# Layer 1's expert blocks staggered on TensorE, and the expert features regrouped so that gate and up rows load in runs of eight

## The chip, the cores and the metric

One core of a Trainium2 chip runs the whole program in one launch. The metric is device time in microseconds (us), the median of three runs. The engines are TensorE (PE; its weight loads are listed apart as PEld), VectorE (DVE), ScalarE (ACT), GpSimd (POOL) and SyncE (SP), whose queue issues nearly all loads. Sixteen DMA engines move the data.

## The reference, cut to what matters

Two transformer layers run on 256 image tokens and, in layer 0, on 256 context tokens as well (D = 1024, everything in float32). Each layer is: modulation, attention, residual and layer norm, then a mixture of 16 experts of which each token uses two. Only the mixture concerns this change:

```
h2    = x * (1 + sc2) + sh2                      # tokens x 1024
gates = top-2 of the best group of 4 experts, normalised   # tokens x 16
g     = h2 @ w_gate[e]                           # 1024 -> 512, per expert
u     = h2 @ w_up[e]                             # 1024 -> 512
a     = silu(g) * u * gate[token, e]
out  += a @ w_down[e]                            # 512 -> 1024
x     = layer_norm(ALPHA * x + g2 * out)
```

The sums over the 1024 features of `g` and `u` may be taken in any order, as long as h2 and the rows of `w_gate` and `w_up` are ordered alike.

## The kernel before, in words

**Slots and blocks.** Experts have fixed capacities. Three experts of each layer are static, the others are sorted by their count of tokens into dynamic slots whose expert number is read from a register when its weights are loaded. A slot is cut into blocks of R = 128, 64 or 32 rows. Layer 1 has fifteen blocks, in this order: e0, e1, e2 (32 rows each, static), d0 (a block of 128 and one of 64), d7 and d9 (32 each), d4 and d3 (64 each), d2 (64 and 32), d1 (128), d5 (64), d8 and d6 (32 each). The number after the d is the slot's index.

**One block in layer 1.** `pick` (L1285) gathers a group's rows, up to 128, out of h2 by a one-hot product into `xt`, features on the partitions. `hidden` then does three things: the products with gate and up, 8 feature chunks (L1235, or L1216 and L1218 where R is 128); a copy of the result out of PSUM to `gu` (L1238) and its transposes (L234); and silu times up on ACT and DVE (L1244 to L1246), which gives `aT`. `down` (L1264, or L1258) multiplies `aT` by `w_down`. `put_out` (L1300 to L1302) scales the rows and splits them into `yh` and `yl`, and `put` (L1320, L1323) adds them to the tokens' residual `xs` by a one-hot product and DVE additions, two token tiles of two halves each, over two PSUM buffers. Below, P stands for the products of a block, T for its transposes, D for its down product.

**Their order.** `step` runs P and T of a block, then `flush`, which does the whole put of the block before, then D, and keeps its own put for the next step. In the code that is: P(i), T(i), put(i-1), D(i), P(i+1), and so on. Tile, the layer that turns this program into engine streams, decides the order on each engine from the order of the code and from an estimate of when each instruction can run, so that an instruction may move ahead of an earlier one that is not ready by that estimate.

**Weights.** An expert's weights are six tiles of 1 MB (gate 2, up 2, down 2), loaded by SP (`expert_load`, L155) into a ring, twelve tiles in layer 1. A load waits until the tile that was loaded twelve before it has been read for the last time, and loads are issued strictly in order. With rows `(k p)`, a partition takes from DRAM one row of 2 KB per feature chunk of gate and up, and one row of 4 KB per chunk of down. The first three experts of layer 1 are loaded early, during its attention.

**h2.** `out_proj` makes h2 by two DVE operations on 128x1024 (L873: subtract the mean, times a row; L879: times the deviation, plus a row). Layer 0 writes h2 to DRAM for gathers, layer 1 splits it into two parts in SBUF. The routing's own operations stand on DVE behind and between them (L875, L876, L885).

Of the kernel before, what the change touches and what calls it, by code (L numbers as in the profile page):

```python
# [142 lines left out]
class K:  # L143
# [686 lines left out]
    def out_proj(self, l, ts, w, oT, rows, h2d, score):  # L830
        nc, wk = self.nc, self.wkb
        for n, t in [(n, t) for n in range(2) for t in ts]:
            c = t // 2
            g1, G2, B2 = [rows[:, 3 * c + i] for i in range(3)]
            cs = slice(512 * n, 512 * n + 512)
            zs = []
            if n:
                zs.append(self.half_T(self.xs[:, t, 0:512], 0))
                bs = self.sm.tile([P, 2, 6], F32, name="bs", tag="bs")
                nc.vector.bn_stats(bs[:, 0], self.xs[:, t, 0:512])  # L840
            ps = self.psum([P, 512], "acc")
# [24 lines left out]
            mv = self.sm.tile([P, 6], F32, name="mv5", tag="mv5")  # L866
            nc.vector.bn_aggr(mv[:, 0:2], bs)
            self.rstd(mv[:, 2:3], mv[:, 1:2], 1, 1e-5)
            nc.vector.tensor_scalar(mv[:, 3:4], mv[:, 0:1], -1.0, None, op0=ALU.mult)

            z = self.xs[:, t, :]
            h2 = wk.tile([P, D], F32, name="h2", tag="h2")
            nc.vector.scalar_tensor_tensor(h2, z, mv[:, 0:1], G2, op0=ALU.subtract, op1=ALU.mult)  # L873
            sc = score[:, t, :]
            nc.vector.scalar_tensor_tensor(sc, bl[:, c, 1], mv[:, 3:4], ps, op0=ALU.mult, op1=ALU.add)  # L875
            nc.vector.scalar_tensor_tensor(sc, sc, mv[:, 2:3], bl[:, c, 0], op0=ALU.mult, op1=ALU.add)  # L876

            e = nc.scalar.activation(sc, sc, AF.Exp, scale=-1.0)
            nc.vector.scalar_tensor_tensor(h2, h2, mv[:, 2:3], B2, op0=ALU.mult, op1=ALU.add)  # L879
            if l == 0:  # L880
                nc.scalar.dma_start(h2d[P * t:P * t + P, :], h2)
            else:
                nc.scalar.copy(self.h2s[0][:, t], h2)
                nc.vector.tensor_sub(self.h2s[1][:, t], h2, self.h2s[0][:, t])
            nc.vector.tensor_scalar(sc, sc, 1.0, None, op0=ALU.add)  # L885
            nc.vector.reciprocal(sc, sc)
            nc.vector.tensor_mul(mv[:, 4:5], mv[:, 3:4], mv[:, 2:3])
            nc.scalar.activation(z, z, AF.Identity, scale=mv[:, 2:3], bias=mv[:, 4:5])
            if last:
                i = nc.scalar.activation(self.junk, self.nhalf[:, 0:1], AF.Sigmoid)  # L890
                self.tc.add_manual_dep(i.ins, e.ins.name, NOSYNC, reason="behind the exponentials")
# [283 lines left out]
    def expert_load(self, l, kind, i):  # L1175
        nc, a = self.nc, self.a
        out = []
        if kind == "d":
            v = nc.sync.value_load(self.ids[0:1, i:i + 1], min_val=0, max_val=NE - 1)
        for nm in ("w_gate", "w_up", "w_down"):  # L1180
            K = 4 if nm == "w_down" else 8
            if kind == "s":
                src = a[nm][l][CAPS[l]["first"] + i].rearrange("(k p) f -> p k f", p=P)
            else:
                src = a[nm][l][bass.ds(v, 1)].rearrange("o (k p) f -> p (o k) f", p=P)
            out.append(self.wload(src, K, 4096 // K))
        return out

# [17 lines left out]
            nc.any.tensor_copy(xt[:, k0:k0 + kb, :], pt)  # L1206
        return xt

    def hidden(self, xt, R, gate, up):

        nc, ep = self.nc, self.ep
        aT = ep.tile([P, 4, R], F32, name="aT", tag="aT")
        if R == 128:
            pg, pu = self.psum([P, 512]), self.psum([P, 512])
            for k in range(8):
                nc.tensor.matmul(pg, xt[:, k, :], gate(k), start=k == 0, stop=k == 7)  # L1216
            for k in range(8):
                nc.tensor.matmul(pu, xt[:, k, :], up(k), start=k == 0, stop=k == 7)  # L1218
            sg = ep.tile([P, 512], F32, name="sg", tag="sg")
            nc.scalar.activation(sg, pg, AF.Sigmoid)  # L1220
            nc.vector.tensor_mul(sg, sg, pg)
            nc.vector.tensor_mul(sg, sg, pu)
            pt = self.psum([P, 4, P], "tr")
            for k in range(4):
                self.tr(pt[:, k, :], sg[:, P * k:P * k + P])
            nc.any.tensor_copy(aT, pt)
            return aT
        W = 8 * R
        q = 512 // W
        ps = self.psum([P, W])  # L1230
# [5 lines left out]
                                 start=k == 0, stop=k == 7, tile_position=(0, R * j), skip_group_check=True)  # L1236
        gu = ep.tile([P, W], F32, name="gu", tag="gu")
        nc.any.tensor_copy(gu, ps)  # L1238
        n = W // P
        pt = self.psum([P, n, 2, q, R], "tr")  # L1240
        for i in range(n):
# [63 lines left out]
    def put(self, ys, R, tok, T):  # L1305
# [5 lines left out]
        dt = self.sp.tile([P, nj, P * T], F32R, name="dt", tag="dt", bufs=1)  # L1311
        for j in range(nj):
            nc.vector.tensor_scalar(dt[:, j], self.const("iota")[:, 0:P * T], tok, m[:, j:j + 1], op0=ALU.is_equal, op1=ALU.mult)
        for t in range(T):
            for n in range(2):
                ps = self.psum([P, 512], "c")
                w = min(W, 512)
                for c in range(512 * n, 512 * n + 512, w):
                    for i in range(2):
                        nc.tensor.matmul(ps[:, c % 512:c % 512 + w], dt[:, c // W, P * t:P * t + P], ys[i][:, c % W:c % W + w],  # L1320
                                         start=i == 0, stop=i == 1, skip_group_check=True)
                x = self.xs[:, t, 512 * n:512 * n + 512]
                nc.vector.tensor_add(x, x, ps)  # L1323

    def moe(self, l, T, h2d, yd, rp, prep):

# [18 lines left out]
        def run(part):  # L1345
            for kind, i, cap in part:
                wg, wu, wd = self.expert_load(l, kind, i)
                for r0, R in cut(cap):
# [4 lines left out]
                        self.hold = g.ins.name  # L1353
                    xt = self.xgT(xg, R)
                    y, out = self.rows_out(R)
                    aT = self.hidden(xt, R, wg, wu)
                    self.down(aT, R, wd, out)
                    self.scatter(y, z, R, yd, NT)
                    b[0] += 1
# [1 line left out]
        def groups(part):  # L1361
# [9 lines left out]
                    n += R  # L1371
            return out

        todo, held = [], []

        def run1(grs, xt0=None, last=False):

            for g in grs:
# [4 lines left out]
                for sc, r0, R, load in g:  # L1383
                    todo.append((xt[:, :, o:o + R], R, load))
                    o += R
            while last and todo:
                step()
            if last:
                flush()

        def step():
            xt, R, load = todo.pop(0)
            if load:
                self.w1 = early.pop(0) if early else self.expert_load(l, *load)
            wg, wu, wd = self.w1
            aT = self.hidden(xt, R, wg, wu)
            flush()
            x, z = [v[:, b[0]:b[0] + 1] for v in ixs]
            b[0] += 1
            y, out = self.put_out(R, z)  # L1400
            self.down(aT, R, wd, out)
            held.append((y, R, x))

        def flush():
            while held:
                self.put(*held.pop(0), T)

        NS = NE - ndyn(l)
        early = [self.expert_load(l, *s[:2]) for s in slots[:NS]] if l else []
# [48 lines left out]
    def overflow(self, l, T, h2d, yd, prep):  # L1458
# [8 lines left out]
        with tc.If(v > 0):  # L1467
# [3 lines left out]
            with tc.For_i(0, NE, 1) as e, tc.tile_pool(name=f"ov{l}", bufs=2) as vp:  # L1471
                fl = vp.tile([1, T], I32, name="fl")
                nc.sync.dma_start(fl, fid[bass.ds(e, 1)])
                for b in range(T):
                    fv = nc.values_load(fl[0:1, b:b + 1], min_val=0, max_val=512)
                    with tc.If(fv > 0):
# [29 lines left out]
                        def part(nm):  # L1506
                            kp = 4 if nm == "w_down" else 8
                            n = 4096 // kp
                            s = a[nm][l][bass.ds(e, 1)].rearrange("o (k p) f -> p (o k) f", p=P)

                            def get(k):
                                w = self.ep.tile([P, n], F32, name="wv" + nm, tag="xt" if kp == 4 else "gu")
                                nc.sync.dma_start(w, s[:, k, :])
                                return w
                            return get
                        aT = self.hidden(xt, P, part("w_gate"), part("w_up"))
                        wd = part("w_down")
                        y, out = self.rows_out(P) if l == 0 else self.put_out(P, ix[1])
                        pss = [self.psum([P, 512]) for _ in range(2)]
# [6 lines left out]
                        if l == 0:  # L1526
                            self.scatter(y, ix[1], P, yd, NT)
                        else:
                            self.put(y, P, ix[0], T)

    def combine_load(self, t, T, yd):
        NT = P * T
# [267 lines left out]
```

## Time and profile before

| | |
|---|---|
| time, median of 3 runs (lowest to highest) | 1067.28 us (1066.06 to 1070.09) |
| the profiled execution: its own time, its span | 1065.16 us, 1063.4 us |
| PE busy | 972.4 us, 91% of the span |
| DVE, ACT busy | 498.5 us (47%), 260.6 us (25%) |
| loads by SP's queue | 267.08 MB, 68.0% of the 16 DMA engines' span |
| mean granted TensorE clock | 0.975 of full speed |

How to read it: busy time is the time in which an engine runs an instruction; matmuls are pipelined and their ends are modelled, so that two of them may overlap in the rows and a busy PE need not be at its peak. The span goes from the first to the last instruction. The mixture of layer 0 takes about 366 us to 641 us of it, that of layer 1 about 823 us to 1050 us.

### The profile page before, as it was taken

How to read it: one execution, taken by the hardware profiler on the slowest of the kernel's cores; microseconds unless marked ns; L12 is line 12 of the kernel's file. 1: busy time of each engine (PE TensorE's matmuls, PEld its weight loads, DVE VectorE, ACT ScalarE, POOL GpSimd, SP SyncE). 2: the span in 40 equal slices, each digit the busy share in tenths (PEclk: the TensorE clock that was granted, in tenths of full speed). 3: DMA queues.
4: the chain of work that ended last, by engine and by line, in shares of the span. 5: the costliest groups of instructions: out<-in, count | busy, mean ns of one | idle time of the engine just before them, and what ended most of it. 6: DMA issues, size and time to landing. Idle time of an engine off the chain costs nothing. (4 is left out here: it accounts for less than half of the span.)

```text
span 1063.4 us, 15563 instructions
## 1 busy us (share of the span) xinstructions
PE 972.4 (91%) x5898; PEld 529.0 (50%) x5898; DVE 498.5 (47%) x1361; ACT 260.6 (25%) x686; POOL 84.5 (8%) x92
## 2 busy tenths in 40 slices
PE   4799999989899899999999887989999999999994
PEld 1566567667444444444344442434654665644542
DVE  2524646675646863110001004789937742533346
ACT  2423243553413111111111111423413111111110
POOL 0000000000101311101111110121002000000001
PEclk9899999999999899999999998999999899999998
DMA  9899761210265399999989988778844693999991
GB/s 332 293 344 337 263 206 39 80 52 29 120 238 218 100 387 391 393 389 354 378 307 379 325 308 308 271 296 341 331 139 146 237 391 122 389 394 393 378 342 57
DMA packets 121482, 287.00 MB, mean 270 GB/s; under 512 B 12449, under 2 KB 27441, under 8 KB 114996
## 3 DMA queue, kind: packets, MB, share of 16 engines
q1 hardware_dynamic: 115856, 267.08, 68.0%
q0 software_dynamic: 4560, 16.13, 4.5%
q10 hardware_dynamic: 980, 2.66, 0.6%
q8 instruction: 51, 0.84, 0.3%
q14 instruction: 35, 0.29, 0.1%
HBM read 279.77 MB, written 8.69 MB: 271 GB/s over the span
## 5 line engine op out<-in xcount | busy, mean ns | idle before, releaser
L1235 PE MATMUL acc<-wring,xt 128*32 128x256 f32 (+1 forms) x1440 | 138.6, 436 | 0.5 <-ACT xt L1206 0.5
L1235 PEld LDWEIGHTS acc<-wring,xt 128*32 128x32 f32 (+1 forms) x1440 | 57.9, 118 | 70.7 <-issue 48.9
L843 PE MATMUL acc<-wring,oT 128*128 128x512 f32 x192 | 88.6, 598 | 0.0
L1264 PE MATMUL acc<-wring,aT 128*32 128x256 f32 (+1 forms) x720 | 69.6, 437 | 10.3 <-DVE aT L1246 9.2
L447 PE MATMUL acc<-swh,hT 128*128 128x384 f32 x192 | 68.3, 356 | 4.0 <-ACT v L569 3.6
L448 PE MATMUL acc<-swl,hT 128*128 128x384 f32 x192 | 67.5, 352 | 0.0
L1323 DVE TENSOR_TENSOR xs<-xs,c 128x512 f32<-128x512 f32 x60 | 40.4, 684 | 56.2 <-PE c L1320 56.1
L449 PE MATMUL acc<-swh,hT 128*128 128x384 f32 x192 | 66.3, 346 | 0.0
L1245 DVE TENSOR_TENSOR sgs<-sgs,tr 128x128 f32<-128x128 f32 (+1 forms) x27 | 8.9, 331 | 108.3 <-ACT sgs L1244 108.2
L511 PE MATMUL acc<-wring,hT 128*128 128x512 f32 x128 | 58.9, 594 | 0.0
L1258 PE MATMUL acc<-wring,aT 128*128 128x512 f32 x128 | 57.4, 599 | 0.4
L1216 PE MATMUL acc<-wring,xt 128*128 128x512 f32 x128 | 56.8, 597 | 0.0
L1218 PE MATMUL acc<-wring,xt 128*128 128x512 f32 x128 | 56.2, 593 | 0.0
L398 PE MATMUL m<-wring,cT 128*32 128x512 f32 x256 | 43.6, 653 | 11.9 <-DMA wring<-in_w_mod_dram 11.9
L843 PEld LDWEIGHTS acc<-wring,oT 128*128 128x128 f32 x192 | 34.2, 191 | 32.7 <-issue 32.3
L1264 PEld LDWEIGHTS acc<-wring,aT 128*32 128x32 f32 (+1 forms) x720 | 27.0, 117 | 40.8 <-issue 16.3
L1238 ACT COPY gu<-acc 128x256 f32<-128x256 f32 (+1 forms) x27 | 12.0, 443 | 121.4 <-PE acc L1235 121.4
L358 POOL TENSOR_TENSOR mv<-ve,nhalf 128x1 f32<-128x1 f32 x12 | 14.7, 1228 | 334.9 <-DVE ve L357 264.6
L447 PEld LDWEIGHTS acc<-swh,hT 128*128 128x128 f32 x192 | 36.4, 190 | 9.6 <-issue 4.5
L1218 PEld LDWEIGHTS acc<-wring,xt 128*128 128x128 f32 x128 | 24.4, 190 | 30.6 <-issue 30.3
L1216 PEld LDWEIGHTS acc<-wring,xt 128*128 128x128 f32 x128 | 23.7, 190 | 28.8 <-issue 28.8
L449 PEld LDWEIGHTS acc<-swh,hT 128*128 128x128 f32 x192 | 36.3, 189 | 3.0 <-issue 3.0
(351 smaller groups left out, 1541.1 us busy)
## 6 DMA issues: line engine op xcount, KB each, us to landing
wring<-in_w_gate_dram SPq DMA_DIRECT2D x58, 1024.0 KB, 14.5
wring<-in_w_up_dram SPq DMA_DIRECT2D x58, 1024.0 KB, 14.3
wring<-in_w_down_dram SPq DMA_DIRECT2D x58, 1024.0 KB, 13.8
wring<-in_w_mod_dram SPq DMA_DIRECT2D x48, 1024.0 KB, 7.0
wring<-in_w_in_even_dram SPq DMA_DIRECT2D x24, 256.0 KB, 4.9
wring<-in_w_in_odd_dram SPq DMA_DIRECT2D x6, 1024.0 KB, 12.5
wring<-in_w_out_even_dram SPq DMA_DIRECT2D x4, 1024.0 KB, 5.0
wring<-yd SPq DMA_DIRECT2D x4, 1024.0 KB, 7.9
```

What stands on the lines that cost most here:

```text
L398: nc.tensor.matmul(ps[32 * j:32 * j + 32, :], lhs(k), w[k][:, 512 * j:512 * j + 512], start=k == 0, stop=k == len(w) - 1, tile_position=(0 ...
L447: mm(ps, xh, wh, start=first, stop=False)
L448: mm(ps, xh, wl, start=False, stop=False)
L449: mm(ps, xl, wh, start=False, stop=last)
L511: self.nc.tensor.matmul(ps, h[:, k, :], w(k), start=k == 0, stop=k == 7)
L843: mm = nc.tensor.matmul(ps, oT[:, k, P * t:P * t + P], w[n](k), start=k == 0, stop=k == 7)
L1216: nc.tensor.matmul(pg, xt[:, k, :], gate(k), start=k == 0, stop=k == 7)
L1218: nc.tensor.matmul(pu, xt[:, k, :], up(k), start=k == 0, stop=k == 7)
L1235: nc.tensor.matmul(ps[R * j:R * j + R, :], xt[:, k, :], src[:, W * jj:W * jj + W], start=k == 0, stop=k == 7, tile_position=(0, R * j), sk ...
L1258: nc.tensor.matmul(ps, aT[:, k, :], w(k)[:, 512 * n:512 * n + 512], start=k == 0, stop=k == 3)
L1264: nc.tensor.matmul(ps[R * j:R * j + R, :], aT[:, k, :], w(k)[:, W * j:W * j + W], start=k == 0, stop=k == 3, tile_position=(0, R * j), ski ...
L1323: nc.vector.tensor_add(x, x, ps)
```

## The change

Two things are changed.

First, the features that an expert sees are regrouped. Feature chunk k held features 128k to 128k+127; now partition p of chunk k holds feature 8p+k. `w_gate` and `w_up` are loaded as `(p k)`: a partition's eight rows are neighbours in DRAM, and a tile of four chunks takes one run of 8 KB per partition where it took four of 2 KB. h2 is written in that order: both DVE operations that make it go over (q, k) with k inside, so that h2 is written, and in the second one read, at a stride of 128 elements, while the other operands stay in their order. This holds for both layers. `w_down` stays as it was.

Second, in layer 1 `hidden` is cut into `products` and the rest, and `step` runs P of a block before T and D of the block before it. `put` is cut into its two token tiles.

```diff
-            nc.vector.scalar_tensor_tensor(h2, z, mv[:, 0:1], G2, op0=ALU.subtract, op1=ALU.mult)
+            hq, rq = "p (k q) -> p q k", "p (q k) -> p q k"
+            nc.vector.scalar_tensor_tensor(h2.rearrange(hq, k=8), z.rearrange(rq, k=8), mv[:, 0:1], G2.rearrange(rq, k=8),
+                                           op0=ALU.subtract, op1=ALU.mult)
...
-            nc.vector.scalar_tensor_tensor(h2, h2, mv[:, 2:3], B2, op0=ALU.mult, op1=ALU.add)
+            nc.vector.scalar_tensor_tensor(h2.rearrange(hq, k=8), h2.rearrange(hq, k=8), mv[:, 2:3], B2.rearrange(rq, k=8),
+                                           op0=ALU.mult, op1=ALU.add)
...
+            rows = "(k p)" if nm == "w_down" else "(p k)"
-                src = a[nm][l][bass.ds(v, 1)].rearrange("o (k p) f -> p (o k) f", p=P)
+                src = a[nm][l][bass.ds(v, 1)].rearrange(f"o {rows} f -> p (o k) f", p=P)
...
-    def hidden(self, xt, R, gate, up):
+    def products(self, xt, R, gate, up):
...
+        return gu
+
+    def hidden(self, gu, R):
...
-        for t in range(T):
+        def tile(t):
...
+        return [lambda t=t: tile(t) for t in range(T)]
...
         def step():
             xt, R, load = todo.pop(0)
             if load:
                 self.w1 = early.pop(0) if early else self.expert_load(l, *load)
-            wg, wu, wd = self.w1
-            aT = self.hidden(xt, R, wg, wu)
-            flush()
             x, z = [v[:, b[0]:b[0] + 1] for v in ixs]
             b[0] += 1
-            y, out = self.put_out(R, z)
-            self.down(aT, R, wd, out)
-            held.append((y, R, x))
+            pipe.append(dict(gu=self.products(xt, R, *self.w1[:2]), R=R, wd=self.w1[2], x=x, z=z))
+            if len(pipe) > 1:
+                rest()
 
-        def flush():
+        def rest():
+            k = pipe.pop(0)
+            if held:
+                held.pop(0)()
+            aT = self.hidden(k["gu"], k["R"])
             while held:
-                self.put(*held.pop(0), T)
+                held.pop(0)()
+            y, out = self.put_out(k["R"], k["z"])
+            self.down(aT, k["R"], k["wd"], out)
+            held.extend(self.put(y, k["R"], k["x"], T))
```

The code's order in layer 1 is now: P(i+1), first token tile of put(i-1), T(i), second token tile of put(i-1), D(i), P(i+2). In layer 0 `hidden(products(...))` is called in one go, so its order is the one before.

## Rows read from the trace of the kernel before

**Rows 1.** Windows, both layers' blocks: window, busy us per engine (count), clock, DMA share, GB/s.
```profile
420.00:600.00 180.00, 168.93 (x991) 79.06 (x989) 16.91 (x36) 24.19 (x50) 23.70 (x24) 1.00 0.99 366
...
860.00:1050.00 190.00, 183.91 (x1240) 99.10 (x1232) 75.66 (x154) 24.66 (x51) 0.00 (x0) 0.99 0.85 320
833.00:860.00 27.00, 24.73 (x334) 16.46 (x330) 21.67 (x84) 3.28 (x8) 0.00 (x0) 0.87 0.96 357
```
**Rows 2.** Lines, PE, 420 to 600: busy us, mean ns, idle before, releaser.
```profile
L234 PE MATMUL tr<-ident,gu 128*128 128x128 f32 x18 | 3.7, 298 | 4.5 <-ACT gu L1238 4.5
```
**Rows 3.** Lines, PE, layer 1's blocks, 860 to 1050, same columns.
```profile
L1264 PE MATMUL acc<-wring,aT 128*32 128x256 f32 (+1 forms) x272 | 29.9, 446 | 3.6 <-DVE aT L1246 2.9 <-PE c L1320 0.7
...
L234 PE MATMUL tr<-ident,gu 128*128 128x128 f32 x32 | 5.5, 280 | 0.0
```
**Rows 4.** Timeline, PE, layer 1: start us, us, what, count, idle before.
```profile
903.45 0.50 PE L1320 MATMUL c<-yh,dt 128*128 128x512 f32 x1
...
904.48 0.60 PE L234 MATMUL tr<-ident,gu 128*128 128x128 f32 x4
904.96 0.50 PE L1320 MATMUL c<-yh,dt 128*128 128x512 f32 x1
...
906.94 3.65 PE L1264 MATMUL acc<-wring,aT 128*64 128x512 f32 x16 [0.65 <-DVE aT L1246]
...
927.60 3.33 PE L1285 MATMUL tr<-ddr,h2s 128*128 128x96 f32 x28
...
946.83 7.04 PE L1235 MATMUL acc<-wring,xt 128*64 128x512 f32 x32
```
**Rows 5.** Timeline, DVE, the same block as the first of rows 4.
```profile
905.54 0.42 DVE L1245 TENSOR_TENSOR sgs<-sgs,tr 128x256 f32<-128x256 f32 x1
905.87 0.68 DVE L1323 TENSOR_TENSOR xs<-xs,c 128x512 f32<-128x512 f32 x1
906.47 0.41 DVE L1246 TENSOR_TENSOR aT<-sgs,tr 128x256 f32<-128x256 f32 x1
```
**Rows 6.** Timeline, PE, layer 1's first blocks.
```profile
835.33 0.44 PE L234 MATMUL tr<-ident,gu 128*128 128x128 f32 x2 [0.51 <-ACT gu L1238]
836.80 1.93 PE L1264 MATMUL acc<-wring,aT 128*32 128x256 f32 x32 [1.03 <-DVE aT L1246]
...
857.58 3.66 PE L1235 MATMUL acc<-wring,xt 128*32 128x256 f32 x64
...
869.36 7.08 PE L1216 MATMUL acc<-wring,xt 128*128 128x512 f32 x16
```
**Rows 7.** Windows, columns as in rows 1: two stretches with a lowered clock.
```profile
849.00:856.00 7.00, 7.00 (x62) 4.22 (x62) 4.35 (x18) 0.58 (x1) 0.00 (x0) 0.51 1.03 394
...
931.00:935.00 4.00, 4.00 (x12) 1.15 (x12) 0.52 (x3) 0.36 (x1) 0.00 (x0) 0.57 1.02 405
```
**Rows 8.** Timeline, SP's queue: start us, us, the load issued.
```profile
867.73 5.36 SPq L155 DMA_DIRECT2D wring<-in_w_down_dram  x2
900.11 1.00 SPq L155 DMA_DIRECT2D wring<-in_w_gate_dram  x2
```
**Rows 9.** Windows, columns as in rows 1: runs of 8 KB, of 4 KB, of 2 KB.
```profile
53.00:58.00 5.00, 5.00 (x33) 3.88 (x32) 0.45 (x1) 1.22 (x4) 0.00 (x0) 1.00 1.05 421
...
947.50:950.50 3.00, 3.00 (x16) 1.00 (x14) 0.99 (x2) 0.62 (x1) 0.00 (x0) 1.00 1.03 407
953.00:961.00 8.00, 7.84 (x41) 3.85 (x36) 3.88 (x9) 0.97 (x2) 0.00 (x0) 1.00 1.05 388
```
**Rows 10.** DMA issues: count, KB each, median us from issue to landing.
```profile
wring<-in_w_out_even_dram SPq DMA_DIRECT2D x4, 1024.0 KB, 5.0
```
**Rows 11.** Instructions of three DVE lines: duration ns min/median/max, first and last start.
```profile
L879 DVE SCALAR_TENSOR_TENSOR h<-h,mv,mid x6: 1278/1278/1280, 323.1 to 812.3; 128x1024 f32<-128x1024 f32 x6
...
L1081 DVE TENSOR_TENSOR gt<-PM,cst x2: 336/336/337, 376.0 to 838.2; 128x169 f32<-128x169 f32 x2
...
L1115 DVE TENSOR_TENSOR big<-PM,cst x2: 442/448/453, 383.3 to 846.2; 128x169 f32<-128x169 f32 x2
```

More of the change, by code (lines that the diff above doesn't have):

```diff
@@ L1181, in expert_load @@
             K = 4 if nm == "w_down" else 8
+            rows = "(k p)" if nm == "w_down" else "(p k)"
             if kind == "s":
-                src = a[nm][l][CAPS[l]["first"] + i].rearrange("(k p) f -> p k f", p=P)
+                src = a[nm][l][CAPS[l]["first"] + i].rearrange(f"{rows} f -> p k f", p=P)
             else:
-                src = a[nm][l][bass.ds(v, 1)].rearrange("o (k p) f -> p (o k) f", p=P)
+                src = a[nm][l][bass.ds(v, 1)].rearrange(f"o {rows} f -> p (o k) f", p=P)
             out.append(self.wload(src, K, 4096 // K))
@@ L1207, in xgT @@
         return xt
-    def hidden(self, xt, R, gate, up):
+    def products(self, xt, R, gate, up):
         nc, ep = self.nc, self.ep
-        aT = ep.tile([P, 4, R], F32, name="aT", tag="aT")
         if R == 128:
@@ L1222, in hidden @@
             nc.vector.tensor_mul(sg, sg, pu)
[L1223 to L1227, printed above, removed]
+            return sg
         W = 8 * R
@@ L1238, in hidden @@
         nc.any.tensor_copy(gu, ps)
+        return gu
+    def hidden(self, gu, R):
+        nc, ep = self.nc, self.ep
+        aT = ep.tile([P, 4, R], F32, name="aT", tag="aT")
+        if R == 128:
+            pt = self.psum([P, 4, P], "tr")
+            for k in range(4):
+                self.tr(pt[:, k, :], gu[:, P * k:P * k + P])
+            nc.any.tensor_copy(aT, pt)
+            return aT
+        W = 8 * R
+        q = 512 // W
         n = W // P
@@ L1355, in run @@
                     y, out = self.rows_out(R)
-                    aT = self.hidden(xt, R, wg, wu)
+                    aT = self.hidden(self.products(xt, R, wg, wu), R)
                     self.down(aT, R, wd, out)
@@ L1372, in groups @@
             return out
+        pipe = []
         todo, held = [], []
@@ L1385, in run1 @@
                     o += R
-            while last and todo:
-                step()
             if last:
-                flush()
+                while todo:
+                    step()
+                rest()
+                for f in held:
+                    f()
         def step():
@@ L1394, in step @@
                 self.w1 = early.pop(0) if early else self.expert_load(l, *load)
-            wg, wu, wd = self.w1
-            aT = self.hidden(xt, R, wg, wu)
-            flush()
             x, z = [v[:, b[0]:b[0] + 1] for v in ixs]
             b[0] += 1
-            y, out = self.put_out(R, z)
-            self.down(aT, R, wd, out)
-            held.append((y, R, x))
-        def flush():
+            pipe.append(dict(gu=self.products(xt, R, *self.w1[:2]), R=R, wd=self.w1[2], x=x, z=z))
+            if len(pipe) > 1:
+                rest()
+        def rest():
[3 more added lines that the diff above has]
+            aT = self.hidden(k["gu"], k["R"])
             while held:
-                self.put(*held.pop(0), T)
+                held.pop(0)()
+            y, out = self.put_out(k["R"], k["z"])
+            self.down(aT, k["R"], k["wd"], out)
+            held.extend(self.put(y, k["R"], k["x"], T))
         NS = NE - ndyn(l)
@@ L1508, in part @@
                             n = 4096 // kp
-                            s = a[nm][l][bass.ds(e, 1)].rearrange("o (k p) f -> p (o k) f", p=P)
+                            rows = "(k p)" if nm == "w_down" else "(p k)"
+                            s = a[nm][l][bass.ds(e, 1)].rearrange(f"o {rows} f -> p (o k) f", p=P)
                             def get(k):
@@ L1515, in part @@
                             return get
-                        aT = self.hidden(xt, P, part("w_gate"), part("w_up"))
+                        aT = self.hidden(self.products(xt, P, part("w_gate"), part("w_up")), P)
                         wd = part("w_down")
@@ L1528, in overflow @@
                         else:
-                            self.put(y, P, ix[0], T)
+                            for f in self.put(y, P, ix[0], T):
+                                f()
     def combine_load(self, t, T, yd):
```

## The prediction

> **What bounds the kernel now.** I read the page's head first, then windows over each stage, then the lines of the mixture, the timelines of PE, DVE and SP, and last the DMA rates. The windows of the blocks show PE busy for 168.93 of 180 us in layer 0 and for 183.91 of 190 us in layer 1, at a clock of 1.00 and 0.99 [rows 1]. In layer 0 the DMA engines are taken up as well (share 0.99); in layer 1 they have 15% free. Both stages are PE's: no line of the mixture there has PE waiting for a weight load. SP instead waits for PE: after the pair of down loads at 867.73 its next load goes out at 900.11, 32 us on, and nothing but a ring slot holds it [rows 8]. So an edit that makes loads faster buys time only if PE would have waited for them, and an edit that reorders PE buys no more than PE's idle time where it stands: 6.1 us in 860 to 1050, of which the down product's line has 3.6 (2.9 behind `aT`, from DVE) and the transposes' line 0.0 [rows 3]. The first blocks are worse off: in 833 to 860 PE has 24.73 of 27 us at a mean clock of 0.87, with DVE at 21.67, because the routing's look-ups, which DVE feeds, share the stretch [rows 1].
>
> **Own time.** The profiled execution took 1065.16 us, 2.1 us below the median of 1067.28. The sum is made on the former and 2.1 us are added at the end.
>
> **Part by part.**
>
> *Loads in runs of 8 KB.* A stretch of 8 KB runs (another weight's) moved 421 GB/s, 4 KB runs 407, the 2 KB runs of gate and up 388 [rows 9]. A gate or up tile of 1 MB falls from 2.70 to 2.49 us, down stays at 2.58; an expert (4 and 2 tiles) from 15.96 to 15.12 us. In layer 0 nothing waits for a load: PE's idle time is behind the copy to `gu` (4.5 us in 420 to 600 [rows 2]) and the like, which stays. Cost 0; at best 1 us back, at worst 0. If I am wrong about the cover, 0.84 us for each of the layer's sixteen experts, 13 us, are at stake; that PE has no DMA wait there is what excludes it.
>
> *The stagger in the steady blocks.* The order in code was P, T, put, D; but the planner had already put half a put ahead of T (903.45, T at 904.48) and the other half behind it (904.96), so the transposes have cover already and show no wait. From P's end to D's start are 903.45 to 906.94, 3.49 us, nearly all put and T; the wait at its end is 0.65 us for `aT` [rows 4]. That wait comes from DVE's queue: silu's product (905.54), then an addition of the put (905.87, 0.68 us), then the product that makes `aT` (906.47) [rows 5]. After the change T still stands between the two halves of a put, silu and `aT` are still made behind T, and the put's addition still stands between them on DVE. Moving P ahead of T covers the copy to `gu`, which was covered. So I take 0; the bounds are 0 and all of the line's idle time, -3.6.
>
> *The start, blocks e0 to e2.* No earlier put is there as cover, and T of e0 waits 0.51 us and D 1.03 us [rows 6]; with P(e1) put ahead of T both go: -1.54. P(e2) (3.66 us, now at 857.58) may also run inside the stretch in which PE is paced by the look-ups. If all of it is hidden, the gain is 1.54 + 3.66 = 5.2; if the planner leaves it behind the look-ups and its gather, and the waits reappear at D(e1), 0. I take -3, near the middle: DVE is at 80% there [rows 1], so it isn't free of charge.
>
> *The clock.* The granted clock was 0.51 over 849 to 856 and 0.57 over 931 to 935, mostly the lower of the two levels (1.2 GHz) [rows 7]: 7 x 0.49 + 4 x 0.43 = 5.1 us lost. Before the first PE ran the chopped look-ups, before the second the gather at 927.60 [rows 4]; a fuller PE may escape one, but both causes stay. I take -1; bounds -5.1 and +3.4 (one more drop such as the first).
>
> *The ring.* This is what the stagger adds. D of a block now runs one P later, so the two slots of its down weights come free later, and loads go strictly in order, so the gate and up loads behind them wait too. I follow it from the end E of D of d0's second block, with all of it worked out from rows as an estimate. A lone tile takes 5.0 us from issue to landing [rows 10], of which 2.3 lie ahead of its 2.70 of transfer. D takes 3.65 us for 64 rows and frees its first slot at E-1.8; d9's two down tiles and d4's gate and up, whose slots are free, then run as one stream from E+0.5: up's first tile lands at 0.5 + 2 x 2.58 + 3 x 2.49 = E+13.1, its second at E+15.6. PE meanwhile has P(d9) 3.66, a stretch of 3.49, D(d7) 1.93 [rows 6] and the gather 3.33: it is ready for P(d4) at E+12.4 and waits 0.7. For d3: two down tiles and three tiles behind E+15.6 land at E+28.2; PE has P(d4) 7.04 from 13.1 [rows 4], 3.49 and D(d9) 1.93, so it is there at E+25.6 and waits 2.6. Behind that the blocks have 64 rows and more, PE needs 7.04 + 3.49 + 3.65 = 14.2 us and the gather for each, and the loads keep up; the last pair of 32-row blocks, d8 and d6, repeats d3's case, 2.6. Sum 5.9 us with PE's order rigid. With 2 KB runs, should the gate and up loads not speed up, the same steps give 1.4 + 3.5 + 3.5 = 8.4. What stands behind the waiting P on PE is T, a put and D of the block before, 3.49 + 1.93 us of ready work; if the planner foresees the wait and moves them ahead, nothing is left. Bounds 0 and +8.4; I take +3, half of the rigid sum.
>
> *h2 at a stride.* Each of the two operations takes 1.28 us on 1024 elements [rows 11]. No row has their strided form. The nearest is a DVE operation on 169 elements: 336 ns with contiguous operands (L1081), 448 with a strided read (L1115), 0.66 ns more per element, 0.68 us on 1024. The pair now has three strided streams, a write in the first and a read and a write in the second. Only the last token tile of each layer lies on the path to the first gather; the others are done while later tiles come from PE. I count the read alone, as that is what the row shows: 2 x 0.68 = +1.4; bounds 0 and, with all three streams, 6 x 0.68 = +4.1.
> The Trainium skill ("SBUF - State Buffer", section "Specifications (TRN2)") speaks against this edit: SBUF has lines of 16 bytes, full rate needs at least two accesses in each line, and every step to a new line costs; at a stride of 128 floats every element is on a new line, for reads and writes alike. The strided read of rows 11 agrees with it, and no run here yet shows a write; by the page's rule the term would be the upper bound, which is the third rival below.
>
> *The end.* The last block now goes P, T, the put before it, D, put, as before. 0, bounds -1.7 and +1.7 (half of a stretch of 3.49 moved to either side). The extra calls in `put` are the same instructions.
>
> Sum: 0 + 0 - 3 - 1 + 3 + 1.4 + 0 = +0.4, so 1065.6 on the profiled execution's scale and **1067.7 us** as a median: no change. What 5.3 us (0.5%) or less moves can't be told from no change in this kernel, so "faster" means below 1061.9 and "slower" above 1072.6.
>
> **The rivals.**
>
> *All of it pays: 1055.9.* The waits for `aT` go (-3.6), P(e2) is wholly hidden at the start (-5.2), most of the lowered clock goes (-4), the loads' 8% keep the ring fed (0), h2 costs 1.4: -11.4. For it: each of these is visible idle or slow time of PE, in the stage that PE bounds, and layer 1 has 15% of the DMA free. Against: three of them must come together, and the `aT` wait is DVE's order, which isn't touched.
>
> *The ring decides: 1075.6, slower.* PE keeps the rigid order and the stream isn't as fast as the rate of another weight says: +8.4, only 1.5 back at the start, clock 0, h2 +1.4: +8.3. It decides as soon as the waits on weights in layer 1 exceed what the start gives by some 4 us. For it: the order in code is what the planner starts from, and SP already sends each load at the moment its slot comes free. Against: 15% free DMA, and large blocks between the small ones that refill the lead.
>
> *Strides cost on writes as well: 1070.4.* +4.1 in place of +1.4. Against it: the tail is partly covered by the routing.
>
> *The change doesn't do what it says: 1068.7.* The planner moves T, put and D ahead of the next P again, since it reckons them ready; then start, clock and ring give 0 and only h2's +1.4 is left. For it: it already reorders puts around T.
>
> **How the numbers follow.** The forecast's case has a chance of 0.32 (0.06 faster, 0.22 the same, 0.04 slower), with its own range of 1062 to 1073; all pays 0.30 (0.28, 0.02, 0); the ring 0.20 (0, 0.04, 0.16); strides 0.08 (0, 0.05, 0.03); the old order 0.10 (0, 0.08, 0.02). Together: faster 0.34, same 0.41, slower 0.25. Of the first rival two fifths lie below 1055 (0.12), of the second two fifths above 1076 (0.08), so 1055 to 1076 leaves out 0.20.
>
> **What would show it.** In PE's timeline, P of the next block (L1235) ahead of the transposes of this one; that settles the last rival. On the down line, the wait for `aT` still near 3 us in 860 to 1050. P(e2) and e2's successor some 3 us earlier against the end of attention. Waits of PE on ring tiles at d4, d3 and d6, of 0.7 to 3 us each. Gate and up stretches near 421 GB/s. The two h2 lines at 1.3 us or at 2 us and more. The clock's two stretches. I am wrong if PE's idle time behind `aT` and at the start falls by more than 6 us with no weight wait in its place, if the weight waits sum to over 7 us, or if layer 0 gains more than 1 us from the faster loads.

## The result and the profile after

| | us | ratio to the kernel before, 95% interval |
|---|---|---|
| kernel before, 8 runs | 1066.65 (1061.97 to 1070.09) | |
| changed kernel, 8 runs | 1074.36 (1070.54 to 1075.05) | 1.0062 [1.0042, 1.0083] |
| changed kernel in a second series, 12 runs | 1071.65 (1067.34 to 1075.98), before there 1066.40 | 1.0043 [1.0023, 1.0063] |

The change makes the kernel slower, by 0.4 to 0.6%. The profiled execution took 1074.58 us (span 1072.8).

Windows of the changed kernel (window, busy us per engine and count, clock, DMA share, GB/s), for [rows 1]:

```profile
833.00:860.00 27.00, 25.56 (x311) 16.39 (x314) 20.68 (x81) 3.07 (x8) 0.00 (x0) 0.76 0.73 285
860.00:1050.00 190.00, 187.08 (x1263) 98.29 (x1255) 74.31 (x152) 24.32 (x50) 0.00 (x0) 0.99 0.82 328
...
420.00:600.00 180.00, 169.60 (x992) 79.51 (x994) 17.06 (x37) 23.64 (x49) 23.71 (x24) 0.99 0.91 353
```

In layer 0 the DMA engines are less taken up than before (0.91 against 0.99), and PE's busy time is nearly the same (169.60 us against 168.93): the faster loads bought nothing there. In layer 1 PE is *busier* (187.08 of 190 us against 183.91) and yet later. The lines of 860 to 1050 (busy us, mean ns | idle before, releaser), for [rows 3]:

```profile
L1278 PE MATMUL acc<-wring,aT 128*32 128x256 f32 (+1 forms) x272 | 34.1, 447 | 2.8 <-DVE aT L1260 2.4 <-issue 0.2
...
L234 PE MATMUL tr<-ident,gu 128*128 128x128 f32 x32 | 5.6, 272 | 0.0
```

The wait for `aT` is nearly what it was (2.4 against 2.9), no line waits for a weight tile, and the loss is not idle time. PE's timeline from 944 to 980 shows what it is (start, us, what, count, idle before); these are blocks whose products and down products stood whole before, d4's down product as in the first fence, d3's products (7.04 us) as in the last line of [rows 4]:

```profile
943.34 3.65 PE L1264 MATMUL acc<-wring,aT 128*64 128x512 f32 x16 [0.53 <-DVE aT L1246]
```
```profile
946.85 1.07 PE L1235 MATMUL acc<-wring,xt 128*64 128x512 f32 x2
...
948.53 1.07 PE L1278 MATMUL acc<-wring,aT 128*64 128x512 f32 x2
...
950.44 1.08 PE L1278 MATMUL acc<-wring,aT 128*64 128x512 f32 x4
...
952.59 1.94 PE L1278 MATMUL acc<-wring,aT 128*64 128x512 f32 x8
954.36 7.03 PE L1235 MATMUL acc<-wring,xt 128*64 128x512 f32 x30
961.23 1.02 PE L1278 MATMUL acc<-wring,aT 128*64 128x512 f32 x2
...
965.67 1.07 PE L1235 MATMUL acc<-wring,xt 128*64 128x512 f32 x2
```

P of d3 lies in two pieces (946.85 and 954.36, from start to the next start 1.00 + 6.87 = 7.87 us, whole it was 7.02), and D of d4 in four (948.53, 950.44, 952.59, 961.23: 1.00 + 1.01 + 1.77 + 0.95 = 4.73 us, whole 3.59), with the put and the gather in between. All through layer 1's mixture, the P and D groups of 32 and 64 rows lie in 45 pieces, against 32 before (26 would be whole).

To compare kernels I use two numbers worked out from traces and runs.

- *PE's time at full clock in layer 1's mixture*, from the first product to the last down product: the times from each matmul's start to the next one's, idle gaps left out, and those under a lowered clock put at the mean of the others of their kind. Before: 203.2 us; changed: 207.2 and, in its second profile, 207.3. Idle gaps: 6.4 us before, 5.4 after. So the mixture costs 4.0 - 1.0 = 3.0 us more by its own order.
- *Time at equal clock.* An execution's time goes with its mean granted clock: a straight line through all 199 timed runs with a recorded clock, one offset per kernel, gives 0.78 us (within 0.07) for each 0.001. At a mean clock of 0.972 the kernel before stands at 1067.1 (within 0.4), the changed one at 1071.0 (1.1) in the first series and 1071.2 (0.9) in the second: **4 us slower**. The rest of the first series' 7.7 us goes with its lower mean clock, 0.968; the kernel before has 0.973 over the 76 of its runs with a recorded clock (its eight of the first series have none). In the second series the changed kernel had 0.9715, the kernel before 0.9723.

### The profile page after: what moved, and what is told of

The parts are those of the page before. It is cut to its first block, busy times and chain, and to the rows that moved or that the text cites. A ratio compares the mean times of both kernels' runs of the same rounds, so it can differ in the third digit from the quotient of the medians.

```text
span 1072.8 us, 15543 instructions
## 1 busy us (share of the span) xinstructions
PE 981.4 (91%) x5898; PEld 529.9 (49%) x5898; DVE 506.7 (47%) x1361; ACT 260.8 (24%) x686; POOL 88.9 (8%) x92
## 5 line engine op out<-in xcount | busy, mean ns | idle before, releaser
L1235 PE MATMUL acc<-wring,xt 128*32 128x256 f32 (+1 forms) x1440 | 143.2, 443 | 0.5 <-ACT xt L1211 0.5
L1278 PE MATMUL acc<-wring,aT 128*32 128x256 f32 (+1 forms) x720 | 76.7, 445 | 10.7 <-DVE aT L1260 10.0
L358 POOL TENSOR_TENSOR mv<-ve,nhalf 128x1 f32<-128x1 f32 x12 | 18.3, 1528 | 337.0 <-DVE ve L357 268.6
## 6 DMA issues: line engine op xcount, KB each, us to landing
wring<-in_w_up_dram SPq DMA_DIRECT2D x58, 1024.0 KB, 15.1
```

What stands on the lines that cost most here:

```text
L1235: nc.tensor.matmul(ps[R * j:R * j + R, :], xt[:, k, :], src[:, W * jj:W * jj + W], start=k == 0, stop=k == 7, tile_position=(0, R * j), sk ...
L1278: nc.tensor.matmul(ps[R * j:R * j + R, :], aT[:, k, :], w(k)[:, W * j:W * j + W], start=k == 0, stop=k == 3, tile_position=(0, R * j), ski ...
```

## The experiments

Ratios are to the kernel before on the same chip and are not quotients of the medians, which are in us. All offsets at equal clock are against 1067.1, or 1066.8 on the chip of the second four.

**The two halves alone.** e1: only the regrouping. e2: only the stagger. e3: the stagger, and the regrouping in layer 1. e4: the regrouping in layer 0. The edits are parts of the diff shown above; in e3 and e4 the layer is tested, as in

```diff
-            rows = "(k p)" if nm == "w_down" else "(p k)"
+            rows = "(k p)" if nm == "w_down" or l != 1 else "(p k)"
```

Expected of e1: 

> The regrouping in both layers (loads in runs of 8 KB, h2 at a stride), without the stagger. Theory A, the clock: in the changed kernel's profile identical work in layer 0 meets four stretches of 3.4 us at a granted clock of 0.50 that the kernel before did not have there (410, 424, 625, and a longer one at 649), some 6.8 us, and where such a stretch falls depends on shifts of a us or two that any edit makes; then this kernel shows other stretches again, between +0 and +6 us (1067 to 1073), and layer 1's blocks cost nothing extra. Theory B, the stagger: the loss is layer 1's order, 3.6 us between its first product and its last down product; then this kernel is at +0.6 (h2's two strided operations on layer 1's path), 1067 to 1068. Theory C, the faster loads: they themselves bring the lowered clock in layer 0; then this kernel has the same stretches at 410, 424 and 625 and +5 to +6, 1072.

Expected of e2: 

> The stagger in layer 1 without the regrouping (rows of 2 KB, h2 as before). Its program is the kernel before's up to layer 1's mixture. Theory A: +0 to +6 by where the clock falls; layer 1's mixture longer by 1 to 2 us apart from the clock. Theory B: +3.6, 1070 to 1071, and the mixture of layer 1 takes 220.7 us from first product to last down product, as in the changed kernel, against 217.1. Theory C: the same +3.6 at most, and no lowered clock in layer 0 where the kernel before has none. If the ring decides with slower loads, PE waits for weight tiles at d4 and d3, 1 to 4 us each.

Expected of e3: 

> The changed kernel with the regrouping in layer 1 alone; layer 0 as before. Theory A: layer 0's clock stretches differ from the changed kernel's; time anywhere between 1067 and 1075. Theory B: +4.2 (3.6 and h2's 0.6 in layer 1), 1070 to 1071. Theory C: layer 0's four stretches gone, 1068 to 1070.

Expected of e4: 

> The kernel before with the regrouping in layer 0 alone. Theory A: anywhere between 1066 and 1073 by the clock, with stretches in other places than in the run with the regrouping in both layers. Theory B: no change, 1066 to 1068 (h2's strided operations of layer 0 are taken back by slack before the first gather). Theory C: lowered clock at 410, 424 and 625 as in the changed kernel, 1071 to 1073.

| | median | ratio | at equal clock |
|---|---|---|---|
| e1 regrouping | 1067.80 | 1.0019 [0.9997, 1.0042] | +0.3 (within 0.9) |
| e2 stagger | 1071.88 | 1.0064 [1.0045, 1.0083] | +3.7 (1.2) |
| e3 stagger, regrouping in layer 1 | 1073.71 | 1.0082 [1.0060, 1.0104] | +3.6 (1.3) |
| e4 regrouping in layer 0 | 1066.55 | 1.0019 [0.9999, 1.0038] | -0.2 (0.9) |

The stagger is the loss (theory B); the regrouping can't be told from nothing. As medians e2 and e3 lie above the 1070 to 1071 of theory B, at equal clock (1070.8 and 1070.7) within it. PE's time at full clock, worked out in the same way to within 0.3 us, agrees: 203.5 us in e1 and 203.7 in e4, 207.7 in e2 and 207.3 in e3. Theory C falls, and with it the reading of the first pair of traces by clock stretches in layer 0. These are the windows 409 to 415 of five profiles, in the order before, changed, e2, e4, and g0, the second profile of the changed kernel; e2's layer 0 is the program of before, e4's that of the changed kernel:

```profile
409.00:415.00 6.00, 5.57 (x57) 2.40 (x55) 3.18 (x9) 0.96 (x2) 0.00 (x0) 1.00 1.04 387
```
```profile
409.00:415.00 6.00, 6.00 (x35) 1.91 (x32) 1.48 (x6) 0.46 (x1) 0.00 (x0) 0.72 1.00 413
```
```profile
409.00:415.00 6.00, 5.57 (x24) 1.73 (x24) 1.90 (x4) 0.18 (x1) 0.00 (x0) 0.72 1.05 388
```
```profile
409.00:415.00 6.00, 5.67 (x55) 2.23 (x55) 3.17 (x9) 0.66 (x2) 0.93 (x1) 1.00 1.00 412
```
```profile
409.00:415.00 6.00, 5.34 (x65) 3.25 (x63) 4.42 (x8) 1.09 (x3) 0.00 (x0) 1.00 1.02 421
```

The clock fell in the changed kernel's first profile and in e2, and not in before, e4 and the changed kernel's second profile, though the loads have runs of 8 KB in the second, fourth and fifth of the windows: a stretch at the lower level (1.2 GHz) comes and goes between executions, behind the same look-ups and transpositions on PE. A single pair of traces differs by several us for that alone.

Whether the stagger also lowers the clock (what is left of theory A) stays open. Over the two series of the changed kernel, e2 and e3, 32 runs, the mean granted clock is 0.970, over the kernel before's 76 runs 0.973; by the line above that is worth some 2.6 us. If it is the stagger's doing, the stagger costs the 5 to 8 us of the medians and not 4. Against it: in e2's profile the clock is lower already in the first 800 us (0.97 against 0.98), where its program is that of the kernel before.

**The price of a cut.** f3 is the kernel before with one 128x128 transposition, its result unused, forced into the middle of each P and each D of 32 or 64 rows in layer 1, 26 in all; f4 has the same 26 behind P's last and ahead of D's first matmul.

```diff
+    def extra(self, i):
+        if self.layer:
+            x = self.tr(self.psum([P, P], "tr"), self.ident)
+            self.tc.add_manual_dep(x.ins, i.ins.name, NOSYNC, reason="extra")
+            return x
...
-                nc.tensor.matmul(ps[R * j:R * j + R, :], xt[:, k, :], src[:, W * jj:W * jj + W],
+                i = nc.tensor.matmul(ps[R * j:R * j + R, :], xt[:, k, :], src[:, W * jj:W * jj + W],
...
+                if x:
+                    self.tc.add_manual_dep(i.ins, x.ins.name, NOSYNC, reason="extra")
+                x = self.extra(i) if k == 3 and j == 2 * q - 1 else None
```

Expected of f3: 

> The kernel before with one extra 128x128 transposition (0.11 us, its result unused) forced into the middle of each P and each D of 32 or 64 rows in layer 1, 26 in all (10 of 64 rows, 16 of 32). Theory cuts: beside 2.9 us for the transpositions, 0.4 to 0.5 us for a cut of 64 rows and 0.3 for one of 32, some 10 us: 1077 to 1080. Rival, cuts are free: 1068 to 1069, equal to the next kernel.

Expected of f4: 

> The same 26 extra transpositions, but behind each P's last matmul and ahead of each D's first, where other full-size work stands anyway: no group is cut. Theory cuts: 2.9 us at most over the kernel before, 1067 to 1069; the difference to the kernel with forced cuts, 8 to 11 us, is the price of 26 cuts. Rival: both the same.

f3 took 1079.47 us, 1.0117 [1.0078, 1.0156]; f4 1068.74, 1.0032 [1.0010, 1.0053]; both as theory cuts expected. The same work costs 10.7 us more inside the groups than beside them (10.5 at equal clock). PE's time at full clock is 215.8 us in f3 and 206.7 in f4, so 9.1 / 26 = 0.35 us a cut; the idle gaps grow from 5.3 to 8.6. (With the planner's own cuts counted, these groups lie in 57 pieces in f3 and 34 in f4, 23 more, which makes 0.40 us a piece.) One 64-row P of f3, and the same one of f4:

```profile
903.48 3.65 PE L1243 MATMUL acc<-wring,xt 128*64 128x512 f32 x16
907.06 0.33 PE L235 MATMUL tr<-ident 128*128 128x128 f32 x1
907.32 3.65 PE L1243 MATMUL acc<-wring,xt 128*64 128x512 f32 x16
910.90 0.50 PE L1335 MATMUL c<-yh,dt 128*128 128x512 f32 x1
```
```profile
899.99 7.09 PE L1244 MATMUL acc<-wring,xt 128*64 128x512 f32 x32
907.00 0.33 PE L235 MATMUL tr<-ident 128*128 128x128 f32 x1
907.09 0.48 PE L1336 MATMUL c<-yh,dt 128*128 128x512 f32 x1
```

From P's start to the put: 7.42 us with the cut, 7.10 without. A transposition after a whole group starts beside its end and holds the next work up by 0.09 us, in the middle by 0.26; and the two pieces take 3.58 us each from their starts to the next start, 7.16 us, where the whole group took 7.01. The matmuls of such a group overlap: the 32 of f4's whole P last 595 ns each on average and take 7.09 us together. That the last ones of a piece have nothing of their kind to overlap with is what I take the price to be; it is argued, the price is measured. The changed kernel's 13 pieces more, at 0.35 to 0.40, make 4.6 to 5.2 us; its PE time grew by 4.0. That its own cuts, by puts and other groups, cost what these transpositions do is an estimate.

**No cuts, by force.** f1 is the changed kernel with every matmul of layer 1's blocks chained in the order of the code; f2 the kernel before with the same chain, and put in two halves around the transposes.

```diff
+    def whole(self, i):
+        if self.chain:
+            if self.chain[-1]:
+                self.tc.add_manual_dep(i.ins, self.chain[-1], NOSYNC, reason="whole groups")
+            self.chain.append(i.ins.name)
+        return i
...
-                nc.tensor.matmul(ps[R * j:R * j + R, :], xt[:, k, :], src[:, W * jj:W * jj + W],
-                                 start=k == 0, stop=k == 7, tile_position=(0, R * j), skip_group_check=True)
+                self.whole(nc.tensor.matmul(ps[R * j:R * j + R, :], xt[:, k, :], src[:, W * jj:W * jj + W],
+                                 start=k == 0, stop=k == 7, tile_position=(0, R * j), skip_group_check=True))
```

Expected of f1: 

> The changed kernel, with every matmul of layer 1's blocks (products, transposes, down, put, gather) held on TensorE in the order of the code, so that no group of products or down products in rows of 32 or 64 is cut by other work. Theory cuts: in the changed kernel's trace such groups lie in pieces (a 64-row P of 7.02 us takes 7.87 in two, a 64-row D of 3.59 takes 4.73 in four), PE's busy time at full clock in layer 1's mixture is 207.2 us against 203.2 with the same instructions, and that is the stagger's cost; then the mixture's busy time falls to 203.5 or less and the time to about 1070. Rival, stagger itself (its longer lead for the loads, its start and its drain): no better than the changed kernel, 1073 to 1075, with new waits in the rigid order. Rival, the clock: a lowered mean clock of the staggered kernels (0.968 to 0.970 against 0.974) is the cost; then 1073 or more unless the clock comes back.

Expected of f2: 

> The kernel before (no stagger, no regrouping) with the same rule, and one half of put placed ahead of the transposes, the other behind them, in the code. Theory cuts: a few cuts of the kernel before go too (down products of e1, d0 and d1, the last products, five in all), some 1.5 us less busy time in the mixture: 1064 to 1066, or the same where the rigid order costs as much in waits at the start. Rival, the planner's interleaving is what hides the waits: rigid order gives 3 to 5 us more, 1069 to 1071.

f1 took 1079.81, 1.0131 [1.0103, 1.0159] (+11.6 at equal clock), *more* than the changed kernel's 1074.36 and 1071.65; f2 1070.63, 1.0039 [1.0019, 1.0059] (+4.1). The 1070 that theory cuts expected of f1 failed, and of the rival the new waits came, at a higher price than its 1073 to 1075; the rival that laid the cost to the clock can't explain +11.6 at equal clock. PE's time at full clock did fall, to 205.4, though not to 203.5, but the idle gaps rose to 15.1 us. Part of them is the wait that the prediction called rigid. f1's lines in the mixture, and its three waits for a weight tile in PE's timeline:

```profile
L1243 PE MATMUL acc<-wring,xt 128*32 128x256 f32 (+1 forms) x672 | 70.3, 450 | 4.4 <-DMA wring<-in_w_up_dram 4.4
L1286 PE MATMUL acc<-wring,aT 128*32 128x256 f32 (+1 forms) x336 | 33.7, 433 | 7.3 <-DVE aT L1268 5.7 <-PE c L1343 1.6
```
```profile
943.30 7.08 PE L1243 MATMUL acc<-wring,xt 128*64 128x512 f32 x30 [1.81 <-DMA wring<-in_w_up_dram]
1038.36 1.93 PE L1243 MATMUL acc<-wring,xt 128*32 128x256 f32 x32 [1.92 <-DMA wring<-in_w_up_dram]
1040.99 1.92 PE L1243 MATMUL acc<-wring,xt 128*32 128x256 f32 x28 [0.69 <-DMA wring<-in_w_up_dram]
```

The waits stand at d3 (943.30) and at the last block, d6, where the prediction had put two of its three. In the changed kernel the same two products, and that of d2, are the ones that lie in pieces. f2 shows the other side, as its rival expected: without the planner's interleaving the kernel before has gaps of 10.3 us instead of 6.4, and its PE time did not fall (204.1 us).

**The loads in the order of use.** g1: the changed kernel, where the down tiles of a dynamic expert are loaded where its down product stands in the code, so behind the next expert's gate and up. g2: the same in f1. g3: the same in e2. g0 is the changed kernel beside them (the second series in the table at the top).

```diff
+            if late and nm == "w_down":
+                w = []
+
+                def down(k, src=src, K=K):
+                    if not w:
+                        w.append(self.wload(src, K, 4096 // K))
+                    return w[0](k)
+                out.append(down)
```

Expected of g0: 

> The changed kernel once more, on the chip of the next three, so that they are compared with it there, and for a second profile of it. 1073 to 1075, 6 to 9 us over the kernel before; PE's busy time in layer 1's mixture again 207 us at full clock. Theory of the clock by execution: stretches of lowered clock in layer 0 in other places than in its first profile, with the mean clock of its runs again near 0.968; if the mean clock comes out at 0.973 or 0.974, like the kernel before's, that part of the loss was chance and the kernel is 4 to 5 us slower, not 8.

Expected of g1: 

> The changed kernel, with the two down tiles of a dynamic expert loaded where its down product stands in the code, behind the next expert's gate and up, so that the loads follow the staggered order of use; the order in which ring slots come free is then the order in which they are asked for. Theory ring: the planner cuts groups of products in the changed kernel because gate and up of the next expert would be late behind the down tiles; with this order the products stay whole (64-row P of d3, d2 and the last 32-row P), PE's busy time in the mixture falls from 207.2 to about 205 and the time by some 2 us against the changed kernel on the same chip. Rival, the cuts come from put and T becoming ready late, not from loads: no change.

Expected of g2: 

> The same load order, with TensorE held in the order of the code (no cuts). In the run with whole groups and the old load order PE waited 4.4 us for up tiles. Theory ring: that wait goes, 4 to 5 us less than there, 1075 to 1076. Rival: the wait is the loads' rate, not their order, and stays: 1079 to 1080.

Expected of g3: 

> The stagger without the regrouping, with the late down loads. If the ring was part of the stagger's cost whatever the rows' length: some 2 us less than the stagger alone (1071.9), 1069 to 1070, still not below the kernel before. If runs of 8 KB are needed to keep the ring fed: no better than 1072, with waits of PE for gate or up tiles.

g0's median of 1071.65 lies below the expected 1073 to 1075, with a mean clock between the two that were to decide; at equal clock it is 4 us slower, as in the first series.

| | median | ratio | at equal clock |
|---|---|---|---|
| g1 changed, down late | 1069.74 | 1.0020 [0.9993, 1.0047] | +3.0 (0.9) |
| g2 whole, down late | 1074.96 | 1.0069 [1.0041, 1.0096] | +5.7 (1.2) |
| g3 stagger only, down late | 1069.15 | 1.0023 [1.0001, 1.0045] | +2.1 (0.9) |

g2 is the clean one: at equal clock it stands 5.9 us below f1 (the medians, from two chips, differ by 4.9), and the wait for up tiles is gone (the products' line in the mixture):

```profile
L1252 PE MATMUL acc<-wring,xt 128*32 128x256 f32 (+1 forms) x672 | 67.9, 449 | 0.0
```

So in the rigid order that wait came from the order of the loads, not from their rate. But g2 is no gain on the changed kernel: with groups whole (204.7 us of PE time) and no weight wait it has some 10 us of idle gaps, 4 more than the kernel before, most of them before D, behind `aT`. No run has whole groups without new waits, so that the cuts are all of the stagger's cost is argued from their count and price. g1 is mixed. Its 64-row products are whole again, as the ring's theory says (35.1 us at full clock for the five blocks, 36.9 in the changed kernel, 35.0 before); but its down products are cut, as here behind two matmuls of d4's, with the put in between:

```profile
954.60 1.07 PE L1287 MATMUL acc<-wring,aT 128*64 128x512 f32 x2
...
956.75 3.65 PE L1287 MATMUL acc<-wring,aT 128*64 128x512 f32 x14
```

That costs 1.00 + 3.58 us where the whole group needs 3.59, and PE's total stays at 207.2, where 205 was expected. At equal clock g1 stands 1.1 us below the changed kernel and g3 1.6 below e2, neither clear of the uncertainty, and neither is below the kernel before. The down products' cuts have a cause of their own. I take it to be that D's `aT` is ready while a put is under way, so that the planner slips D in; that is argued from the order, and no run takes it away alone.

## Why the prediction was right and wrong

The sum was +0.4 us, "no change", at 1067.7; the measured medians, 1074.36 and 1071.65, lie inside the range of 1055 to 1076, the first above the likeliest case's own range (1062 to 1073) and, by the prediction's own bound of 1072.6, slower, the second no change. At equal clock +4 was measured. That both lie inside is owed to a range of 21 us; the steps were off by more than the sum. By its steps:

- *Loads in runs of 8 KB, 0:* right. e4 is -0.2 at equal clock, and the DMA engines' share in layer 0 fell to 0.91 with PE's busy time within 0.7 us of 169.
- *h2 at a stride, +1.4:* near by luck. I counted one strided stream of 0.68 us in each layer. Each of the two operations grew by 0.7 us, the one that only writes at a stride as much as the one that reads and writes so (duration ns min/median/max, before and changed, for [rows 11]); layer 0 paid nothing (e4), and layer 1 for both:

```profile
L873 DVE SCALAR_TENSOR_TENSOR h<-xs,mv,mid x6: 1274/1276/1276, 321.3 to 810.6; 128x1024 f32<-128x1024 f32 x6
```
```profile
L875 DVE SCALAR_TENSOR_TENSOR h<-xs,mv,mid x6: 1977/1990/2008, 319.9 to 816.3; 128x1024 f32<-128x1024 f32 x6
```
```profile
L882 DVE SCALAR_TENSOR_TENSOR h<-h,mv,mid x6: 1973/2014/2031, 322.3 to 818.6; 128x1024 f32<-128x1024 f32 x6
```

  The third rival, 0.68 for each of three streams, fails by the second operation: two streams in one (2014 ns) cost hardly more than one (1990). The Trainium skill ("SBUF - State Buffer", section "Specifications (TRN2)") has the rule that a step to a new line of 16 bytes costs; for writes the trace agrees (1990 against 1276 ns). On layer 1's path both operations count: PE waits 1.66 us for the routing's `sel` where it waited 0.57, 1.1 us more.

```profile
819.76 1.69 PE L212 MATMUL acc<-onesb,identb 128*128 128x512 bf16 x7 [0.57 <-DVE sel L973]
```
```profile
826.82 1.69 PE L212 MATMUL acc<-onesb,identb 128*128 128x512 bf16 x7 [1.66 <-DVE sel L977]
```

- *Steady blocks, 0:* right for the waits, as the lines showed, and wrong in what was counted. I priced idle time alone. PE's order decides its busy time too, since a group of 32 or 64 rows costs 0.35 us more for each time that it is cut, and this term was missing.
- *The start, -3:* wrong in size; about 1 us of waits came back. Up to P(d0a) PE waited 2.2 us before (0.51, 1.03 and 0.64 at a look-up) and 1.2 after. In the changed kernel P(e1) does stand ahead of T(e0), and the 0.51 us are gone, but D(e0) waits 1.21 us for `aT`, since nothing was left between T and D; and P(e2), which I had run inside the look-ups, does two small pieces at 848.60 and 849.32 and its remaining 60 matmuls after them, at 859.09. Rows for [rows 6]:

```profile
845.20 0.44 PE L234 MATMUL tr<-ident,gu 128*128 128x128 f32 x2
846.85 1.93 PE L1278 MATMUL acc<-wring,aT 128*32 128x256 f32 x32 [1.21 <-DVE aT L1260]
848.60 0.59 PE L1235 MATMUL acc<-wring,xt 128*32 128x256 f32 x2
...
849.32 0.62 PE L1235 MATMUL acc<-wring,xt 128*32 128x256 f32 x2
...
859.09 4.55 PE L1235 MATMUL acc<-wring,xt 128*32 128x256 f32 x60
...
871.61 7.08 PE L1220 MATMUL acc<-wring,xt 128*128 128x512 f32 x16
```

  That P(d0a) starts at 871.61, only 2.3 us later than before although layer 1's first product started 5.8 later, is no gain: D(e2) is still to come there.
- *The ring, +3:* the mechanism was right and its form wrong. With PE's order rigid the wait was 4.4 us (5.9 predicted), at d3 (1.8, predicted 2.6) and d6 (2.6, predicted 2.6), and none at d4 (0.7 predicted). In the changed kernel the planner fills the waits by D and put, as I had hoped, but by cutting P: 1.9 us for the 64-row products. "Nothing is left" was the wrong end for that case.
- *The clock, -1:* wrong in kind. It was read from stretches of one execution, and these differ between executions by more than the term. The two stretches that it names stayed: from 820 to 960 the granted clock is 0.94 in both profiles.

Put together, the measured parts give PE's time +4.0, its gaps in layer 1's mixture -1.0 and the routing +1.1, so +4.1 against +4 at equal clock (uncertain by about 1). Beside the forecast of +0.4, the cost of reordering was missing (+4.0) and the gains at the start (2 us of 3) and of the clock (1) did not come, while the weight waits that it allowed for (3) stayed away. The rivals' totals don't tell causes here: 1075.6, the slower rival, is nearest to the first series, and 1070.4, strides on writes, to the 1071 at equal clock, and neither mechanism was what cost the time. Of the slower rival it is shown that weights come late when PE's order is rigid (f1, g2); that lateness made the planner cut the 64-row products is likely, since they are whole in g1, but with that taken away other groups were cut and the time is not clearly better.

## What to carry to other kernels

Idle time is not all that an order costs: where matmuls of 32 or 64 rows overlap on TensorE, count the pieces of such groups in the timeline before and after, and price each piece by the same group whole. Before a pipeline is given one more stage, put its loads in the new order of use (5.9 us between f1 and g2); but check first whether the planner had already overlapped the stages. A difference of a few us between two traces is compared at equal granted clock, over many runs, before it is explained.

## What was not expected of the hardware

- A cut of a 32- or 64-row group costs 0.35 us of PE time on average (9.1 us for 26), and up to 1.0 us where it falls behind the first two matmuls of a 64-row down product.
- A DVE operation on 128x1024 with two strided SBUF streams takes 2.01 us, with one 1.99, with none 1.28.
- The mean granted clock of one and the same kernel differs from 0.967 to 0.978 between executions, and its time with it (1062 to 1074 us for e1).
